# Queries of the dilation-4 pattern: from projections inside attention to seven half-size block products ahead of it

## Chip, core and metric

The kernel runs on one core of a Trainium2 chip. The metric is the device time of one execution in microseconds (us), and smaller is better. All inputs and outputs are float32. TensorE (PE in the profile) multiplies, ScalarE (ACT) and VectorE (DVE) do the elementwise work, GpSimd (POOL) and SyncE (SP) mostly issue DMA transfers.

## What is computed

Two decoder layers, 1024 tokens wide and 1024 features deep. The first layer mixes tokens with a gated MLP, the second with dilated sliding-window attention; each is followed by an MLP of width 4096 with a squared ReLU. The change touches the attention layer alone. Cut to that:

```python
B_HEADS, B_HEAD_DIM = 16, 64
B_PATTERNS = ((128, 1), (512, 4), (2048, 16))          # (window, dilation), numbered g = 0, 1, 2

def mixer_b(h, w_qkv, w_out, slopes):
    qkv = (h @ w_qkv).reshape(B, S, N_PAT, 3, B_HEADS, B_HEAD_DIM)
    for g, (window, dilation) in enumerate(B_PATTERNS):
        o, lse = dilated_branch(qkv[:, :, g, 0], qkv[:, :, g, 1], qkv[:, :, g, 2], window, dilation, slopes)
        ...
    wts = softmax(stack(lses)); o = sum(wts * stack(outs))
    return o.reshape(B, S, 1024) @ w_out

def dilated_branch(q, k, v, window, dilation, slopes):
    ...                                   # tokens are split by residue modulo the dilation, 128 per block
    s = einsum(q, k and the previous block's k) * E ** -0.5 + ALiBi bias, masked
    m = max(s); p = exp(s - m); l = sum(p)
    return (p / l) @ v, m + log(l)
```

For each of the three patterns there is a q, a k and a v, each a product of h (1024 x 1024) with 1024 columns of `w_qkv`. So there are nine such products: (g, X) with X = 0 for q, 1 for k and 2 for v.

## The kernel before, in words

**Split numbers.** To keep float32 accuracy every operand of a large product is cut in two tiles of a faster PE type, a rounded `hi` (an ACT cast, line 111) and the rest `lo` (a DVE subtraction, line 112); the helper is `split`. A product then takes three matmuls: hi by hi, hi by lo, lo by hi.

**Stage "values".** Five of the nine products are made by `values` before attention starts: v of all three patterns, and q and k of pattern 0. Each is cut into half-size blocks and made by seven block products in place of eight (Strassen's scheme in Winograd's form): `V_STEPS` lists (g, X, p) with p the product's number. One entry of `V_STEPS` is 4 row blocks m x 4 k tiles x 3 terms = 48 matmuls with 512 columns each (line 1502). `RightForms.prepare` loads and splits the weight block of the next entry; `evict` takes a finished sum out of PSUM. Products 1, 5 and 6 are only kept for later sums; 2, 3, 4 and 7 give a quarter of the result each. A finished quarter of v is split and written to `v_dram`, one of q or k to `qk_dram`, 512 KB a block, by a DMA from POOL's queue (line 1474), and attention reads it back.

**Stage "attention".** For each pair of heads hp (eight pairs) and each pattern in the order 2, 1, 0, `attend` puts the work into numbered slots, eight slots to a pattern, so that a pair takes 24. A slot has two positions, here called half slots. In a pattern's slots: scores (PE, tile `sc`), then `soften`: bias and minimum on DVE (line 1728, tile `p`) and the exponential on ACT (line 1730); transposes of the probabilities on PE (tile `pT`); `halve`, a cast on ACT and a subtraction on DVE that split the transposed probabilities (`pThi`, `pTlo`); and `weighted`, the product with v (tile `pv`), three half slots behind the transposes. `merge` weighs the three patterns' results of an earlier pair on DVE (tile `bc`). The stretch of pattern 0 carries most of this DVE work.

**Projections inside attention.** The other four products, q and k of patterns 2 and 1, are made pair by pair by the generator `project`: a unit is one (pattern, q or k) of one pair, 2 halves x 8 steps, and a step is three matmuls with 512 columns (line 1605, tiles `psq` and `psk`). At a unit's start `cut` splits the next unit's 128x1024 weights (tiles `wqk_hi`, `wqk_lo`), at each half's end the sum is split into `qhi`/`qlo` or `khi`/`klo`. `lead` steps run before slot 0. After that a running credit lets out a step now and then, after the attention work of a half slot:

```python
credit += 512 - lead
while credit >= 351:
    credit -= 351
    next(stream, None)
```

With 512 steps in all and a lead of 56 that is 456/351 = 1.30 steps a half slot. These steps are what PE does while ACT and DVE work on scores and probabilities. The scheduler places instructions by its own estimates near the place where the slots issue them, and every engine takes its instructions in a fixed order.

**After the last pair's projections** the first products with the output weights (`out_begin`, tile `psoa`) take their place, from slot 176 on.

## Time and profile before

| | |
|---|---|
| median of 3 runs | 2651.45 us (2650.08 to 2653.6) |
| the profiled execution | 2647.53 us, of which the span of its instructions is 2645.8 |
| granted TensorE clock | 0.999 of full speed |
| PE busy | 2624.9 us, 99% of the span, 13016 matmuls |
| DVE busy | 1982.6 us, 75% |
| ACT busy | 1397.5 us, 53% |
| stage "values" | from 943.3 us of the span to 1331.2 |
| stage "attention" | from 1331.2 to about 1985 |

"Busy" is the time in which an engine had an instruction in work; matmuls overlap in the pipeline, so a busy PE says that it had no hole, not that it ran at its peak. The chain is followed back from the last instruction to what released each step. A row with `[1.46 <-ACT p L1730]` says that the engine sat idle for 1.46 us before this instruction, and that the ACT instruction of line 1730 ended the wait. In a window's row the number in brackets counts instructions. Tiles carry the names of the program without numbers.

### The profile page before, as it was taken

The page shows a single profiled execution, that of the slowest core. Times are in us where ns is not written, and L with a number is a line of the kernel's source. Part 1 is how long each engine was busy: PE and PEld are TensorE (multiplying, and loading weights), DVE is VectorE, ACT ScalarE, POOL GpSimd, SP SyncE. Part 2 cuts the span into 40 slices and gives each one's busy share as a digit, 9 for nine tenths or more (in the row PEclk, how much of TensorE's full clock was granted, in tenths as well). Part 3 has the DMA queues.
Part 4 walks back from the last instruction along what each step waited for, and adds up shares of the span by engine and source line. Part 5 has one row for each costly group of instructions (what it writes and reads, how often), then busy time and mean ns, then how long its engine had stood idle before and what let it go on. Part 6 is the DMA issues. An engine that isn't in the chain of part 4 may idle for free.

```text
span 2645.8 us, 36898 instructions
## 1 busy us (share of the span) xinstructions
PE 2624.9 (99%) x13016; PEld 2183.0 (83%) x13016; DVE 1982.6 (75%) x3558; ACT 1397.5 (53%) x2639; POOL 110.2 (4%) x190
## 2 busy tenths in 40 slices
PE   8999999999999999999999999999999999999998
PEld 6888888888888878888888888888888888888887
DVE  6886898886988887646647777777669965687887
ACT  5454475555444554343436666666657655554432
POOL 0000000000000001111110000000010000000000
PEclk9999999999999999999999999999999999999999
DMA  8543367778867546555576655665893654495562
GB/s 299 187 121 118 128 198 238 241 235 283 315 215 243 190 159 231 190 184 191 175 217 165 169 157 142 159 156 155 251 247 120 212 191 147 154 324 185 180 207 88
DMA packets 351794, 513.74 MB, mean 194 GB/s; under 512 B 60140, under 2 KB 185684, under 8 KB 351608
## 3 DMA queue, kind: packets, MB, share of 16 engines
q1 hardware_dynamic: 335176, 452.61, 54.9%
q0 software_dynamic: 16432, 58.76, 6.2%
q8 instruction: 102, 1.67, 0.3%
q14 instruction: 84, 0.69, 0.1%
HBM read 374.34 MB, written 136.95 MB: 193 GB/s over the span
## 4 chain that ended last, share of the span: by engine, by line
PE 94%; DVE 3%; DMA 1%; ACT 1%; issue 0%; SPq 0%; POOL 0%; DVEq 0%; ACTq 0%; POOLq 0%
PE psd L1154 23%; PE psua L987 13%; PE psv L1502 13%; PE psq L1605 7%; PE psk L1605 7%; PE psuc L987 7%; PE psd_wout L432 3%; PE psu L774 3%; PE psub L987 3%; PE psv L528 3%; PE pv L1788 3%; PE sc L1708 2%; PE pT L1761 2%; PE sc L1704 1%; PE psoa L1992 1%; PE pT L1764 1%
## 5 line engine op out<-in xcount | busy, mean ns | idle before, releaser
L987 PE MATMUL psua<-right,left 128*128 128x512 f32 x1536 | 362.8, 390 | 0.1
L1154 PE MATMUL psd<-rhi,lhi 128*128 128x512 f32 x880 | 342.9, 390 | 0.0
L1154 PE MATMUL psd<-rhi,llo 128*128 128x512 f32 x880 | 342.1, 389 | 0.0
L1154 PE MATMUL psd<-rlo,lhi 128*128 128x512 f32 x880 | 342.0, 389 | 0.0
L987 PEld LDWEIGHTS psua<-right,left 128*128 128x128 f32 x1536 | 287.2, 188 | 61.3 <-DVE left L112 0.7
L1730 ACT ACTIVATE p<-p,stat 128x128 f32<-128x128 f32 (+1 forms) x384 | 168.7, 441 | 70.8 <-DVE stat L1728 69.7
L1154 PEld LDWEIGHTS psd<-rhi,lhi 128*128 128x128 f32 x880 | 165.2, 188 | 35.1 <-ACT part L1018 0.9
L1154 PEld LDWEIGHTS psd<-rhi,llo 128*128 128x128 f32 x880 | 165.2, 188 | 34.1
L1154 PEld LDWEIGHTS psd<-rlo,lhi 128*128 128x128 f32 x880 | 165.2, 188 | 33.9
L987 PE MATMUL psuc<-right,left 128*128 128x512 f32 x768 | 186.5, 390 | 0.0
L987 PEld LDWEIGHTS psuc<-right,left 128*128 128x128 f32 x768 | 143.7, 188 | 30.3 <-DVE right L112 0.6
L112 DVE TENSOR_TENSOR pTlo<-pT,pThi 128x512 fp32r<-128x512 f32 (+1 forms) x160 | 99.6, 622 | 69.3 <-ACT pThi L111 67.5
L112 DVE TENSOR_TENSOR left<-ws,left 128x512 fp32r<-128x512 f32 x128 | 88.0, 689 | 81.7 <-ACT left L111 79.9
L112 DVE TENSOR_TENSOR llo<-lraw,lhi 128x1024 fp32r<-128x1024 f32 x112 | 136.2, 1218 | 2.3 <-ACT lhi L111 2.3
L1605 PE MATMUL psk<-form_L,wqk_hi 128*128 128x512 f32 x384 | 126.3, 410 | 0.0
L1605 PE MATMUL psq<-form_L,wqk_hi 128*128 128x512 f32 x384 | 125.1, 406 | 0.0
L111 ACT CAST lhi<-lraw 128x1024 fp32r<-128x1024 f32 x112 | 117.0, 1048 | 11.8 <-PE psd L1154 6.7
L111 ACT CAST pThi<-pT 128x512 fp32r<-128x512 f32 (+1 forms) x160 | 84.9, 530 | 71.6 <-PE pT L1761 51.9
L111 ACT CAST left<-ws 128x512 fp32r<-128x512 f32 x128 | 79.2, 620 | 79.6 <-DVE ws L911 69.0
L1502 PE MATMUL psv<-vrhi,form_S 128*128 128x512 f32 x384 | 119.8, 390 | 1.3 <-DVE vpart L1467 0.9
L1728 DVE CUSTOM_DVE_ANT_0 p<-sc,bias 128x128 f32<-128x128 f32 (+1 forms) x384 | 113.8, 346 | 9.0 <-PE sc L1708 5.4
L138 DVE SCALAR_TENSOR_TENSOR adaacc<-adaw,silu_c,adaacc 128x512 f32<-128x512 f32 x140 | 104.5, 747 | 7.3 <-DMA adaw<-in_ada_w_dram 6.2
(369 smaller groups left out, 6099.4 us busy)
## 6 DMA issues: line engine op xcount, KB each, us to landing
lraw<-forms SPq DMA_DIRECT2D x112, 512.0 KB
adaw<-in_ada_w_dram SPq DMA_DIRECT2D x160, 256.0 KB
up<-in_mlp_w_up_dram SPq DMA_DIRECT2D x64, 512.0 KB
forms<-s SPq DMA_DIRECT2D x128, 256.0 KB
rraw<-in_mlp_w_down_dram SPq DMA_DIRECT2D x64, 512.0 KB
forms<-part SPq DMA_DIRECT2D x96, 256.0 KB
v<-vs POOLq DMA_DIRECT2D x48, 512.0 KB, 3.6
vraw<-in_b_w_qkv_dram SPq DMA_DIRECT2D x42, 512.0 KB
```

The costliest lines, as they stand in the source:

```text
L111: first = A.copy(hi, src) if hi_engine is A else hi_engine.tensor_copy(hi, src)
L112: return first, lo_engine.tensor_tensor(lo, src, hi, op=ALU.subtract)
L138: ins = V.scalar_tensor_tensor(acc[:], raw[:], silu_c[:, k : k + 1], acc[:], ALU.mult, ALU.add)
L432: T.matmul(p[:], stat[a][:, k, o : o + P], u[b][:, w], start=n == 0, stop=n == count - 1)
L528: ins = T.matmul(sums[i][:], hT[half][a_][:, k, o : o + P], units[c, k // 2][b_][:, n : n + HALF], start=k + a_ + b_ == 0, stop=k == KD - ...
L774: T.matmul(p[:], wu[a_][:, k * P : (k + 1) * P], hT[half][b_][:, k, :], start=k + a_ + b_ == 0, stop=k == KD - 1 and a_ == 1)
L987: T.matmul(acc, w[:, a, k, :], right[p][:, b, k, :], start=p in (1, 2, 5) and k + a + b == 0, stop=k == 3 and a == 1, skip_group_check=True)
L1154: ins = T.matmul(sums[kind, m][:, w], l[a][:, k, m * P : (m + 1) * P], r[b][:, k, w], start=p in (1, 5, 2, 3) and kp + k + a + b == 0 or b ...
L1502: T.matmul(acc, rows[:, m * P : (m + 1) * P], cols_, start=p in (1, 2, 5) and kp + k + a + b == 0, stop=kp == 1 and k == 1 and a == 1, ski ...
L1605: T.matmul(p[:], wu[a][:, k * P : (k + 1) * P], h_op(k, half, b), start=k + c_ == 0, stop=k == KD - 1 and c_ == 2)
L1728: V.tensor_tensor_reduce(out=pr, in0=banks[e][:, sl], in1=st["bias"][:, width - w :], scale=-0.125, scalar=3e38, op0=ALU.add, op1=ALU.min, ...
L1730: A.activation(pr, pr, AF.Exp, bias=nm, scale=-1.0, accum_out=l)
```

## The change

q of pattern 1 moves from `project` to `values`. It becomes a sixth product of seven entries in `V_STEPS`, (1, 0), between v of pattern 0 and q of pattern 0. Its quarters are split in the order of residues that pattern 1 uses (`"p (i r) -> p r i"`) and written to a third plane of `qk_dram`. In attention, `load_q` fetches the two halves (128 x 1024 each, `qhi` and `qlo`) seven slots before the pair's pattern 1 starts, on SP's queue, and `place_of` finds a tile's columns in the stored order. `project` is left with six units for two pairs where it had eight: 384 steps, a lead of 48, and 336/348 = 0.97 steps a half slot.

```diff
-    qk_dram = dram.tile([N_PAIRS, 2, P, 2, S], F32, name="qk_0")
+    qk_dram = dram.tile([N_PAIRS, 3, P, 2, S], F32, name="qk_0")
...
-    V_STEPS = [(g, X, p) for g, X in ((2, 2), (1, 2), (0, 2), (0, 0), (0, 1)) for p in (1, 2, 5, 6, 7, 4, 3)]
+    V_STEPS = [(g, X, p) for g, X in ((2, 2), (1, 2), (0, 2), (1, 0), (0, 0), (0, 1)) for p in (1, 2, 5, 6, 7, 4, 3)]
...
-                    t = (work if m % 2 else parted).tile([P, 2, HALF], F32R, name=f"qs_{X}_{p}_{m}", **where)
-                    split(t[:, 0], t[:, 1], acc)
-                    nc.gpsimd.dma_start(qk_dram[4 * dh + m, X, :, :, half * HALF : (half + 1) * HALF], t[:].bitcast(F32))
+                    t = (work if m % 2 else parted).tile([P, 2, HALF], F32R, name=f"qs_{g}_{X}_{p}_{m}", **where)
+                    hi, lo = t[:, 0], t[:, 1]
+                    if g == 1:
+                        hi, lo, acc = (z.rearrange(way, r=4) for z, way in ((hi, "p (r i) -> p r i"), (lo, "p (r i) -> p r i"), (acc, "p (i r) -> p r i")))
+                    split(hi, lo, acc)
+                    nc.gpsimd.dma_start(qk_dram[4 * dh + m, X + 2 * g, :, :, half * HALF : (half + 1) * HALF], t[:].bitcast(F32))
...
-                todo = [(n, X) for n in range(len(order)) if order[n][1] for X in range(2)]
+                todo = [(n, X) for n in range(len(order)) if order[n][1] for X in range(order[n][1] % 2, 2)]
...
+                if g == 1:
+                    @at(max(0, base - 7), 1)
+                    def load_q():
+
+                        for i, m in enumerate(("qhi", "qlo")):
+                            t = my[m] = qk[1].tile([P, S], F32R, name=f"{m}_{hp}_{g}", tag=m)
+                            nc.sync.dma_start(t[:].bitcast(F32), qk_dram[hp, 2, :, i, :])
...
-                                T.matmul(banks[e][:, sl], q_[a][rows, tq], k_[b][rows, keys],
+                                T.matmul(banks[e][:, sl], q_[a][rows, tq if g == 2 else place_of(t)], k_[b][rows, keys],
...
+                def place_of(t):
+                    start = (t % 2) * HALF + (t // 2) * P
+                    return slice(start, start + P)
...
-            lead, credit = 7 * KD, 0
+            lead, credit = 6 * KD, 0
...
-                    credit += 512 - lead
-                    while credit >= 351:
-                        credit -= 351
+                    credit += 384 - lead
+                    while credit >= 348:
+                        credit -= 348
```

Over the whole program PE has 9373 rows of instructions before and 9345 now, and 13002 and 12954 matmuls in them. How the change moves instructions shows at three places.

**PE, pattern 0 of the third pair** (heads 4 and 5), from the last group of scores on (`sc_4_0_3`, `sc_5_0_3`). `psq`/`psk` are projection steps, `pv` the products with v. Before:

```order
L1704 MATMUL sc_5_0_3_14128<-bk_2_3_14037,bq_2_3_14036 128x256 x2
L1605 MATMUL psq_3_1_0_14081<-form_L22_8464,wqk_14_hi_13710 128x512 x2
L1605 MATMUL psq_3_1_0_14081<-form_L22_8464,wqk_14_lo_13711 128x512
L1605 MATMUL psq_3_1_0_14081<-form_L22_8464,wqk_14_hi_13710 128x512 x2
L1605 MATMUL psq_3_1_0_14081<-form_L22_8464,wqk_14_lo_13711 128x512
L1788 MATMUL pv_4_0_0_14161<-pThi_4_0_0_14106,v_2_0_13873 128x256
```

Now:

```order
L1715 MATMUL sc_5_0_3_14465<-bk_2_3_14380,bq_2_3_14379 128x256 x2
L1608 MATMUL psk_3_1_1_14366<-form_L12_7979,wqk_11_hi_14068 128x512 x2
L1608 MATMUL psk_3_1_1_14366<-form_L12_7979,wqk_11_lo_14069 128x512
L1803 MATMUL pv_4_0_0_14497<-pThi_4_0_0_14443,v_2_0_14225 128x256
L1803 MATMUL pv_4_0_0_14497<-pTlo_4_0_0_14444,v_2_0_14225 128x256
```

Two projection steps stood between these scores and the next product with v, and one stands there now. The transposes that need these scores' exponentials (`pT_4_0_2`) follow one more step behind, in both.

**SP's queue, the load of q for the third pair.** Names are tiles and the tensors in memory. Before, at the place where the weights of the fourth pair's q of pattern 1 were fetched:

```order
L1673 DMA bq_1_3_13093<-qk_0_118 64x2x256 x2
L1582 DMA wq_3_1_raw_13236<-in_b_w_qkv_dram 128x8x128
L1671 DMA bk_2_0_13750<-qk_0_118 64x2x256 x2
L1899 DMA o_dram_11204<-bc_0_2_12581 128x1024
L1650 DMA v_2_2_13256<-v_2_117 64x8x256
```

Now, where the stored q of the third pair is fetched:

```order
L1684 DMA bq_1_2_13411<-qk_0_118 64x2x256 x4
L1661 DMA qhi_2_1_13742<-qk_0_118 128x1024
L1661 DMA qlo_2_1_13744<-qk_0_118 128x1024
L1647 DMA v_1_0_13343<-v_0_115 128x8x256
L1838 DMA st_dram_11737<-stat_1_1_13074 128x8x4
```

The loads of a pair's q stand in the queue among the second pair's pattern 0, ahead of that pattern's v (`v_1_0`); the weight load is gone.

**PE, the last pair (heads 14 and 15), where the projections end.** Before:

```order
L1761 MATMUL pT_14_2_0_18244<-ident_76,p_14_2_2_18026 128x128 x2
L1605 MATMUL psk_7_1_0_18227<-form_L22_8464,wqk_31_hi_17803 128x512 x2
L1605 MATMUL psk_7_1_0_18227<-form_L22_8464,wqk_31_lo_17804 128x512
L1605 MATMUL psk_7_1_0_18227<-form_L22_8464,wqk_31_hi_17803 128x512 x2
L1605 MATMUL psk_7_1_0_18227<-form_L22_8464,wqk_31_lo_17804 128x512
```

Now:

```order
L1608 MATMUL psk_7_1_0_18184<-form_L22_8464,wqk_23_lo_17709 128x512
L1776 MATMUL pT_14_2_0_18326<-ident_76,p_14_2_0_18098 128x128 x2
L1776 MATMUL pT_14_2_0_18326<-ident_76,p_14_2_2_18119 128x128 x2
L1776 MATMUL pT_14_2_1_18360<-ident_76,p_14_2_4_18256 128x128 x2
L1776 MATMUL pT_14_2_1_18360<-ident_76,p_14_2_6_18292 128x128 x2
L1719 MATMUL sc_14_1_0_18370<-khi_7_1_18010,qhi_7_1_18157 128x128
L1803 MATMUL pv_14_2_0_18350<-pThi_14_2_0_18335,v_7_2_18040 128x128
```

The last projection now ends ahead of these transposes, and no projection step stands between them, the first scores of pattern 1, and the product with v that needs their split.

## Prediction

> **What bounds the kernel now.** I read the page's busy line and chain first, then the table of windows for the stage "values" and for one whole pair of attention (the third), then the longest piece of the chain there and the list of what PE waited for between 1331 and 2022 us.

> ```profile
> span 2645.8 us, 36898 instructions
> PE 2624.9 (99%) x13016; PEld 2183.0 (83%) x13016; DVE 1982.6 (75%) x3558; ACT 1397.5 (53%) x2639; POOL 110.2 (4%) x190
> PE 94%; DVE 3%; DMA 1%; ACT 1%; issue 0%; SPq 0%; POOL 0%; DVEq 0%; ACTq 0%; POOLq 0%
> 1179.00:1255.00 76.00, 76.00 (x337) 62.94 (x336) 43.98 (x50) 31.63 (x43) 10.61 (x16) 1.00 0.56 191
> 1255.00:1331.00 76.00, 76.00 (x337) 62.90 (x337) 45.96 (x56) 33.26 (x47) 13.20 (x19) 1.00 0.57 198
> 1532.54:1605.76 73.22, 73.22 (x486) 62.92 (x486) 53.98 (x166) 48.19 (x143) 3.04 (x6) 1.00 0.58 153
> 1331.37 10.88 PE psq L1605 x48
> PE pT L1764 <- ACT p L1730: 1.5, 1, 1.5
> PE pst L893 <- ACT h L897: 0.3, 1, 0.3
> ```

> A window's columns are its bounds and length, then the busy time of PE, PEld, DVE, ACT and POOL, the granted clock, the DMA share and GB/s. PE is the chain (94%), and in both stages it is busy for the whole window at a clock of 1.00. In all of attention it waited once, 1.5 us, for an exponential. So matmuls taken out are time taken out, as long as ACT and DVE still deliver. The piece of 48 matmuls with 512 columns in 10.88 us gives 0.2267 us for one, and 0.68 for a projection step of three. The two windows of "values" give 152 / 674 = 0.2255: the same price.

> **The matmuls.** Attention loses q of pattern 1: 8 pairs x 2 halves x 8 steps x 3 = 384 matmuls, 384 x 0.2267 = 87.04 us. "Values" gains seven products of 48: 336 x 0.2267 = 76.16 us. The balance is 48 matmuls, -10.88 us. The other 12954 stay.

> **What the added products bring to "values".** Rows of the tile that they fill, of its stores, and of the slowest DVE operation there is with a strided operand:

> ```profile
> L1502 PE MATMUL psv<-form_L,vrhi x192: 389/389/389, 1178.9 to 1319.9; 128*128 128x512 f32 x192
> L1474 POOL DMA_DIRECT2D qk<-qs x32: 675/681/707, 1195.9 to 1335.0; - x32
> 1541.90 1.09 DVE L1884 TENSOR_TENSOR bc<-oT,bc 128x512 f32<-128x512 f32 x1 [1.65 <-DMA bc<-w_dram]
> ```

> All 192 matmuls of that form, in q and k of pattern 0, take 389 ns with no spread: the stage runs at PE's pace. Those two windows are two such products, and the new one repeats their work, so its splits, sums and copies fall in a stretch where DVE has 76 - 46 = 30 us idle and ACT 43. The split in residue order has strides. Its 16 subtractions cost between 0.69 us (the plain price, below) and 1.09 (the strided row) each, so 6.4 us more at most, in 30 of idle time. Sixteen more stores of 512 KB on POOL's queue come at the rate at which 32 went out in the 152 us, DMA share 0.57. Cost: nothing, covered by matmuls; without that cover the worst case is the 6.4 us.

> **What attention loses beside matmuls.** The third pair's stretch of pattern 0 is the densest, and I cut it in five windows:

> ```profile
> 1550.80:1556.90 6.10, 6.10 (x47) 5.14 (x47) 4.14 (x15) 3.79 (x14) 0.81 (x2) 1.00 0.14 29
> 1556.90:1563.00 6.10, 6.10 (x40) 5.30 (x39) 5.42 (x13) 3.04 (x7) 0.00 (x0) 1.00 0.53 151
> 1563.00:1569.10 6.10, 6.10 (x39) 5.36 (x38) 5.61 (x14) 5.16 (x14) 0.00 (x0) 1.00 0.64 190
> 1569.10:1575.20 6.10, 6.10 (x40) 5.36 (x39) 5.58 (x15) 5.10 (x14) 0.00 (x0) 1.00 0.74 196
> 1575.20:1581.30 6.10, 6.10 (x40) 5.36 (x39) 4.53 (x14) 4.71 (x13) 0.00 (x0) 1.00 0.59 190
> L111 ACT CAST qhi<-psq x32: 559/578/589, 1336.9 to 1886.0; 128x512 fp32r<-128x512 f32 x32
> L112 DVE TENSOR_TENSOR qlo<-psq,qhi x32: 679/691/693, 1337.5 to 1886.7; 128x512 fp32r<-128x512 f32 x32
> 1564.27 1.22 DVE L112 TENSOR_TENSOR wqk_lo<-wk_raw,wqk_hi 128x1024 fp32r<-128x1024 f32 x1
> 1562.49 1.06 ACT L111 CAST wqk_hi<-wk_raw 128x1024 fp32r<-128x1024 f32 x1 [0.44 <-PE sc L1704]
> 1579.01 0.69 DVE L112 TENSOR_TENSOR pTlo<-pT,pThi 128x512 fp32r<-128x512 f32 x1 [1.50 <-ACT pThi L111]
> ```

> The DVE sum is 25.28 of 30.5 us, the ACT sum 21.80. Per pair the change removes 48 matmuls, two `qhi`/`qlo` and one weight split: on PE 10.88 us, on DVE 2 x 0.69 + 1.22 = 2.60, on ACT 2 x 0.58 + 1.06 = 2.22. Spread evenly, the stretch has 30.5/73.2 of that. PE's time there becomes 30.5 - 4.53 = 26.0, DVE's work 25.28 - 1.08 = 24.2 (93%), ACT's 21.80 - 0.92 = 20.9. So PE stays the longest, but by 1.8 us only, where DVE's idle time was 5.2. Part of that idle time lies behind PE and shrinks with it; part, like the 1.50 us before the last row, is DVE standing in its order behind an ACT result. If just that 1.50 stays, DVE needs 25.7 of 26.0 and nothing stalls. If all 5.2 stays, 29.4 against 26.0: a stall of 3.4 us. These are the ends for one pair.

> Inside that stretch the tightest place is the fourth transpose of a pack right behind the last scores. Here it is in the third pair, with two projection steps before the products with v, and in the seventh, with one:

> ```profile
> 1579.47 1.20 PE L1704 MATMUL sc<-bk,bq 128*128 128x256 f32 x8
> 1581.66 0.41 DVE L1728 CUSTOM_DVE_ANT_0 p<-sc,bias 128x256 f32<-128x256 f32 x1
> 1582.12 0.51 ACT L1730 ACTIVATE p<-p,stat 128x256 f32<-128x256 f32 x1 [1.77 <-DVE stat L1728]
> 1583.40 0.27 PE L1764 MATMUL pT<-ident,p 128*128 128x128 f32 x1
> ...
> 1873.89 1.20 PE L1704 MATMUL sc<-bk,bq 128*128 128x256 f32 x8
> 1876.31 0.51 ACT L1730 ACTIVATE p<-p,stat 128x256 f32<-128x256 f32 x1
> 1877.12 0.27 PE L1764 MATMUL pT<-ident,p 128*128 128x128 f32 x1
> ```

> In the third pair the exponential is done at 1582.63 and the transpose comes at 1583.40: slack 0.77. The order shows one step fewer there now, 0.68 us, which leaves 0.1. The seventh pair already stands at one step: done at 1876.82, transpose at 1877.12, slack 0.3 and no wait. But both DVE rows come at their times after a stretch of DVE work, and that stretch is to be shortened by 4.5 us against 1.1 of work. So I expect small waits, between 0 and 3.4 us a pair. The seventh pair's row is the nearest and speaks for the low end; I take 0.5, in each of the seven pairs that still have projections: +3.5 us. I leave the one wait of before as it is:

> ```profile
> 1431.19 1.20 PE L1704 MATMUL sc<-bk,bq 128*128 128x256 f32 x8
> 1432.16 1.05 ACT L111 CAST wqk_hi<-wq_raw 128x1024 fp32r<-128x1024 f32 x1 [1.98 <-PE sc L1704]
> 1434.93 0.41 DVE L1728 CUSTOM_DVE_ANT_0 p<-sc,bias 128x256 f32<-128x256 f32 x1
> 1435.39 0.51 ACT L1730 ACTIVATE p<-p,stat 128x256 f32<-128x256 f32 x1 [1.21 <-DVE stat L1728]
> 1436.04 0.33 PE L1764 MATMUL pT<-ident,p 128*128 128x128 f32 x1 [1.46 <-ACT p L1730]
> ```

> It is the first pair, at the same place with one step. A weight split waited 1.98 us on ACT, the casts behind it in ACT's order came late, DVE waited for those with `qlo` and `pTlo`, and the bias step stood behind them: 3.74 us from scores to bias where the third pair had 2.19. This is how a 1.5 us stall arises with ACT and DVE far from full.

> [...]

> **The last pair's end of projections.** In the order, the last steps no longer stand between its first transposes and the products with v that need their split. Three rows of the third pair give that chain:

> ```profile
> 1536.73 0.60 PE L1761 MATMUL pT<-ident,p 128*128 128x128 f32 x4
> 1537.42 0.59 ACT L111 CAST pThi<-pT 128x512 fp32r<-128x512 f32 x1 [0.66 <-PE pT L1761]
> 1538.04 0.69 DVE L112 TENSOR_TENSOR pTlo<-pT,pThi 128x512 fp32r<-128x512 f32 x1 [0.57 <-ACT pThi L111]
> ```

> From the transposes' start to the end of `pTlo` it is 2.0 us, and 0.6 of it is the transposes themselves. Scores of pattern 1 cover some of the rest. The ends are 0 and 2.0; I take 1.0.

> **Queues.** The two 512 KB loads of q go on SP's queue seven slots ahead, 7 slots of 62.3/24 us with the shorter pairs, 18 us. No row shows such a load; the store of the same size, by the page's group of DMA issues, and a chain of two small DMAs bound it from below and above:

> ```profile
> qk<-qs POOLq DMA_DIRECT2D x32, 512.0 KB, 4.3
> 1531.59 0.35 DVE L1863 TENSOR_TENSOR ma<-ma,mal 128x16 f32<-128x16 f32 x3
> ```

> A store lands 4.3 us after issue; the merge's way through memory and back takes from 1531.94 to 1541.90, 10 us. Two loads one behind the other are 8.6 to 10 us, in 18: hidden. What stands behind them on SP, v of pattern 0, is used a pattern (62.3/3 = 21 us) later. If the cover were gone, first scores of pattern 1 would wait. The merge row itself waits 1.65 us now and would wait some 1.5 longer with shorter slots; that is DVE at a place with idle time, and costs nothing.

> **Sum.** -87.04 + 76.16 + 3.5 + 1.0 = -6.4 us against the profiled execution of 2647.53 us, so 2641.1. That execution lies 3.9 us under the median of 2651.45, and I apply the difference to the median: 2645.0. No change can be told from noise within 0.2%, 5.3 us.

> **Rivals.**
> 1. Full gain. The seventh pair's slack of 0.3 speaks for it: all pairs then stand at one step without a wait, and the first pair's 1.46 may go, as one split fewer stands in ACT's order. -10.9 to -12.3: 2639 to 2640.5.
> 2. My forecast, stalls of 0 to 1 us a pair: -10.9 to -3.
> 3. Small stalls grow: 1.2 to 1.6 us a pair, as in the first pair, with the last pair's 1: 7 x 1.4 + 1 = 10.8, no change, 2651.
> 4. Slower: DVE becomes the bound of pattern 0's stretch. Its idle time behind ACT stays whole, 3.4 us a pair: 7 x 3.4 + 1 - 10.9 = +13.9, 2665. It decides from 10.88 / 7 = 1.55 us a pair. The windows at 5.4 to 5.6 of 6.1 speak for it; that of the three pairs that run with one step there (first, fourth, seventh) only the first stalls, against.

> That the change moves nothing on PE is excluded: the order holds 48 matmuls fewer.

> **How the numbers follow.** Forecast 0.5, full gain 0.2, small stalls 0.2, slower 0.1. The forecast is the second, 2645.0; alone it ranges 2640.5 to 2648.5. A range from 2639 to 2652 holds the first three but for their tails, 0.85, and leaves the fourth out. Faster by over 5.3 us: all of the first and 0.35 of the second's 0.5, 0.55. Slower by as much: the fourth and no more, 0.1. Within: 0.35.

> **What would show it.** "Values" longer by 76 us with no hole in PE; a pair's period of 73.22 - 10.88 = 62.3 plus its stall; PE rows of the fourth transpose behind the last scores of pattern 0 with waits of 0 to 1 us on ACT's exponentials; a wait of PE on `pTlo` in the last pair; no wait on `qhi` or `qlo`. I am wrong if pairs take 64 us or more (the third and fourth rivals), if "values" grows by over 77, or if scores of pattern 1 wait for a DMA.

## The result and the profile after

The changed kernel takes 2662.57 us in the median of six runs (2657.89 to 2663.86), the kernel before 2649.34 beside it (six runs, 2647.74 to 2653.6). The ratio is 1.0046, with a 95% interval of 1.0033 to 1.0059: it is slower by some 12 us, where 6.4 less were forecast. The profiled execution is the quickest of the six, 2657.89 us, 10.4 over that of before; the trace readings that follow account for those 10.4. Why the other five take 4 to 6 us more isn't recorded: their mean clocks are the same (0.998 and 0.999).

The page after, its span, busy line and chain:

```profile
span 2656.2 us, 36952 instructions
PE 2622.6 (99%) x12968; PEld 2175.2 (82%) x12968; DVE 2006.8 (76%) x3584; ACT 1416.2 (53%) x2657; POOL 115.8 (4%) x206
...
PE 85%; DVE 6%; ACT 3%; DMA 3%; issue 1%; SPq 0%; POOL 0%; DVEq 0%; ACTq 0%; POOLq 0%
```

PE's share of the chain fell from 94% to 85%. DVE, ACT and DMA took the difference: PE now waits. By windows, three of "values" (the first is the added product), then two middle pairs and the step from the seventh pair to the last, each from the first scores of pattern 0 to the next pair's:

```profile
1178.00:1254.00 76.00, 76.00 (x337) 62.94 (x336) 46.95 (x49) 36.14 (x43) 10.61 (x17) 1.00 0.56 192
1254.00:1330.00 76.00, 76.00 (x337) 62.91 (x336) 46.61 (x53) 32.11 (x43) 11.04 (x17) 1.00 0.57 197
1330.00:1406.00 76.00, 76.00 (x337) 62.94 (x336) 44.84 (x55) 32.62 (x47) 13.17 (x19) 1.00 0.56 193
1607.64:1671.80 64.16, 62.99 (x440) 53.98 (x439) 50.81 (x163) 46.42 (x140) 2.19 (x6) 1.00 0.73 196
1671.80:1736.61 64.81, 63.68 (x444) 54.38 (x442) 51.05 (x164) 45.81 (x140) 2.22 (x6) 1.00 0.67 173
1865.34:1937.07 71.73, 69.25 (x459) 59.05 (x457) 50.32 (x165) 45.10 (x141) 4.58 (x8) 0.98 0.99 271
```

"Values" paid 76.2 us and has no hole. Attention got back 66.8 us in place of 87.0. Where the other 20.3 went, by the matmuls that the order leaves out of each stretch, at 0.2267 us:

| stretch (from first scores of pattern 0 to the next pair's) | before | now | matmuls alone would give | lost |
|---|---|---|---|---|
| from the end of "values" to the first pair's | 81.1 | 68.8 | 68.2 | 0.6 |
| first to second pair | 75.1 | 66.9 | 64.9 | 2.1 |
| second to seventh pair, five periods | 367.7 | 323.0 | 312.6 | 10.5 |
| seventh to last pair | 75.2 | 71.7 | 66.4 | 5.3 |
| last pair's pattern 0, to the first `psod` (output products) | 43.5 | 45.3 | 43.5 | 1.8 |

With 0.8 us gained ahead of "values" and 1.8 lost behind attention: -0.8 + 76.2 - 66.8 + 1.8 = +10.4.

What PE waited for in attention and behind it, waits over 0.15 us (in before one of 1.5 us stood there, and one of 0.3). `bq` and `bk` are q and k of pattern 0, read back from memory; `stat` is the minimum that the bias step leaves for the exponential:

```profile
PE pT L1779 <- ACT p L1745: 4.9, 5, 1.7
PE pv L1803 <- DVE pTlo L112: 4.8, 12, 1.0
PE pv L1803 <- ACT pThi L111: 1.5, 3, 1.1
PE sc L1715 <- DMA bq<-qk: 0.8, 1, 0.8
PE pst L893 <- ACT acc L274: 0.8, 1, 0.8
PE sc L1715 <- issue: 0.6, 1, 0.6
```

Twenty waits on transposed or exponentiated probabilities, of 0.15 to 1.7 us, of two kinds. Up to the first `psod` all waits make 13.4 us, 12.0 more than before; with 1.7 us for a lower clock (below) that is 13.7 of the 20.3. The other 6.6 us stand in no wait of this list. The first kind stands at pattern 0's last scores, here in the second pair (DVE, ACT and PE rows in order of time):

```profile
1557.67 1.20 PE L1715 MATMUL sc<-bk,bq 128*128 128x256 f32 x8
1558.95 0.68 DVE L112 TENSOR_TENSOR bc<-bc,bc 128x512 fp32r<-128x512 f32 x1
1559.66 0.69 DVE L1813 TENSOR_TENSOR oT<-oT,pv 64x512 f32<-64x512 f32 x1
1560.38 0.69 DVE L112 TENSOR_TENSOR klo<-psk,khi 128x512 fp32r<-128x512 f32 x1
1560.99 0.68 DVE L112 TENSOR_TENSOR pTlo<-pT,pThi 128x512 fp32r<-128x512 f32 x1
1561.59 0.41 DVE L1743 CUSTOM_DVE_ANT_0 p<-sc,bias 128x256 f32<-128x256 f32 x1
1562.05 0.51 ACT L1745 ACTIVATE p<-p,stat 128x256 f32<-128x256 f32 x1 [1.51 <-DVE stat L1743]
1562.70 0.33 PE L1779 MATMUL pT<-ident,p 128*128 128x128 f32 x1 [1.17 <-ACT p L1745]
```

The scores are ready at 1558.87. DVE takes four other operations ahead of the bias step, without a gap, and that step starts 2.7 us later; PE has two projection steps and a product with v for that time, and then waits. The second kind stands between a transpose and the product with v that needs its two halves, here behind the first pair:

```profile
1506.96 0.39 PE L1803 MATMUL pv<-pThi,v 128*128 128x256 f32 x1 [1.10 <-ACT pThi L111]
1507.80 0.39 PE L1803 MATMUL pv<-pTlo,v 128*128 128x256 f32 x1 [0.46 <-DVE pTlo L112]
```

Two things make it new. One is the cover: the PE work between the last transpose of a group of three or four and the first use of their low half, counted at 0.2267 us for 512 columns. At the tightest place of a pattern it was usually 2.78 us in pattern 2, 3.34 in pattern 1 and 3.46 in pattern 0. In the first seven pairs it is 2.10 to 2.83, 1.98 to 2.66 and 2.78 now, mostly one projection step (0.68) less. (The figures in the expectations below are up to 0.3 higher; the differences are the same.) The other is the chain through ACT and DVE. It takes 2.0 us when nothing is in its way, 1.4 of it behind the last transpose, and the cover left would still have done for that, but for one place in the last pair. At the twelve places where PE waited, it took 2.6 to 6.1 us, and 2.0 to 4.4 at the same places before: the cast or the subtraction stood behind other work in its engine's order. The 1.10 us above follow an idle ACT and then eight exponentials in a row; the longest wait on `pTlo`, 1.03 us at 1595.17, follows a DVE that had waited for the merge weights:

```profile
1502.76 0.40 ACT L1745 ACTIVATE p<-p,stat 128x128 f32<-128x128 f32 x1 [3.92 <-DVE stat L1743]
...
1592.26 1.06 DVE L1899 TENSOR_TENSOR bc<-oT,bc 128x512 f32<-128x512 f32 x1 [3.22 <-DMA bc<-w_dram]
```

The last pair has both, and something else. PE's rows there, and the granted clock in windows of 5 us:

```profile
1905.36 0.39 PE L1608 MATMUL psk<-form_L,wqk_lo 128*128 128x512 f32 x1
1905.59 1.04 PE L1776 MATMUL pT<-ident,p 128*128 128x128 f32 x8
1906.81 0.32 PE L1719 MATMUL sc<-khi,qhi 64*128 64x128 f32 x1 [0.19 <-ACT khi L111]
1907.30 0.33 PE L1803 MATMUL pv<-pThi,v 128*128 128x128 f32 x1 [0.17 <-ACT pThi L111]
...
1908.25 0.33 PE L1803 MATMUL pv<-pTlo,v 128*128 128x128 f32 x1 [0.16 <-DVE pTlo L112]
...
1910.49 0.79 PE L2007 MATMUL psoa<-wo_hi,oTs 128*128 128x512 f32 x1
```

```profile
1905.00:1910.00 5.00, 4.48 (x37) 3.65 (x35) 3.41 (x10) 3.27 (x9) 0.40 (x1) 0.96 1.00 363
1910.00:1915.00 5.00, 5.00 (x23) 4.11 (x21) 2.13 (x13) 2.63 (x12) 0.00 (x0) 0.70 1.13 254
```

After the last projection PE has only small pieces of work for 4 us, some of them behind short waits, 0.5 us in all. Then the granted clock falls, and a `psoa` matmul (output product) takes 0.79 us. (0.04 + 0.30) x 5 = 1.7 us are lost by the clock alone.

### The profile page after: what moved, and what is told of

It reads as the page before. It is cut to its first block, busy times and chain, and to the rows that moved or that the text cites. A ratio compares the mean times of both kernels' runs of the same rounds, so it can differ in the third digit from the quotient of the medians.

```text
span 2656.2 us, 36952 instructions
## 1 busy us (share of the span) xinstructions
PE 2622.6 (99%) x12968; PEld 2175.2 (82%) x12968; DVE 2006.8 (76%) x3584; ACT 1416.2 (53%) x2657; POOL 115.8 (4%) x206
## 4 chain that ended last, share of the span: by engine, by line
PE 85%; DVE 6%; ACT 3%; DMA 3%; issue 1%; SPq 0%; POOL 0%; DVEq 0%; ACTq 0%; POOLq 0%
PE psd L1154 23%; PE psv L1505 16%; PE psua L987 13%; PE psuc L987 7%; PE psk L1608 4%; PE psd_wout L432 3%; PE psu L774 3%; PE psub L987 3%; PE psv L528 3%; PE psq L1608 2%; PE pv L1803 2%; ACT p L1745 2%; PE sc L1719 1%; PE pT L1776 1%; DVE pTlo L112 1%
## 5 line engine op out<-in xcount | busy, mean ns | idle before, releaser
L1154 PE MATMUL psd<-rlo,lhi 128*128 128x512 f32 x880 | 342.0, 389 | 0.0
L112 DVE TENSOR_TENSOR left<-ws,left 128x512 fp32r<-128x512 f32 x128 | 87.9, 688 | 81.0 <-ACT left L111 79.2
L112 DVE TENSOR_TENSOR llo<-lraw,lhi 128x1024 fp32r<-128x1024 f32 x112 | 136.1, 1218 | 2.3 <-ACT lhi L111 2.3
L112 DVE TENSOR_TENSOR pTlo<-pT,pThi 128x512 fp32r<-128x512 f32 (+1 forms) x160 | 98.9, 619 | 39.0 <-ACT pThi L111 37.4
L111 ACT CAST lhi<-lraw 128x1024 fp32r<-128x1024 f32 x112 | 117.1, 1048 | 11.5 <-PE psd L1154 6.7
L111 ACT CAST left<-ws 128x512 fp32r<-128x512 f32 x128 | 79.2, 620 | 81.9 <-DVE ws L911 70.1
L1505 PE MATMUL psv<-form_S,vrhi 128*128 128x512 f32 x384 | 118.1, 389 | 0.0
L111 ACT CAST rhi<-rraw 128x1024 fp32r<-128x1024 f32 x48 | 50.5, 1052 | 110.9 <-issue 64.5
## 6 DMA issues: line engine op xcount, KB each, us to landing
lraw<-forms SPq DMA_DIRECT2D x112, 512.0 KB
up<-in_mlp_w_up_dram SPq DMA_DIRECT2D x64, 512.0 KB
rraw<-in_mlp_w_down_dram SPq DMA_DIRECT2D x64, 512.0 KB
vraw<-in_b_w_qkv_dram SPq DMA_DIRECT2D x50, 512.0 KB
v<-vs POOLq DMA_DIRECT2D x48, 512.0 KB, 3.6
```

Source lines behind the costliest of these rows:

```text
L111: first = A.copy(hi, src) if hi_engine is A else hi_engine.tensor_copy(hi, src)
L112: return first, lo_engine.tensor_tensor(lo, src, hi, op=ALU.subtract)
L1154: ins = T.matmul(sums[kind, m][:, w], l[a][:, k, m * P : (m + 1) * P], r[b][:, k, w], start=p in (1, 5, 2, 3) and kp + k + a + b == 0 or b ...
L1505: T.matmul(acc, rows[:, m * P : (m + 1) * P], cols_, start=p in (1, 2, 5) and kp + k + a + b == 0, stop=kp == 1 and k == 1 and a == 1, ski ...
```

## Experiments

In the experiments, as in the changed kernel, the period of a middle pair is the mean of the five from the second pair to the seventh. It is 64.6 us in the changed kernel; from before, with the matmuls taken out, it would be 62.5.

**Is it the transfers, or DVE's load?** Theory A made DVE's work and order responsible, theory B the added transfers. Two kernels that each leave something out:

```diff
-steps = [lambda f=f, g=g, half=half: f(g, half) for f, g in pieces for half in range(2)]
+steps = [(lambda f=f, g=g, half=half: f(g, half)) if f is cut or hp > N_PAIRS - 3 else (lambda: None) ...]
```

> The multiplications and additions of the merge are left out in the first six pairs (ten of twelve DVE operations, some 8 us of DVE a pair; the split of the merged rows and all transfers stay). Theory A: both DVE waits go, pair periods fall from 64.4-65 to 62.3-63, 10 to 13 us in six pairs, and the last pair keeps its 5 us: 2649 to 2653 us, ratio 1.000 to 1.0015. Theory B (transfers): nothing changes, 2662, ratio 1.0046.

```diff
 for i, m in enumerate(("qhi", "qlo")):
+    if hp:
+        my[m] = got[1][m]
+        continue
     t = my[m] = qk[1].tile(...)
     nc.sync.dma_start(...)
```

> The loads of the stored q are left out for all pairs but the first, whose q tiles the others use; nothing else changes. Theory B (the added transfers slow attention): pair periods fall from 64.4-65 towards 62.3, 8 to 12 us in all, ratio 1.000 to 1.0015. Theory L: pairs two to seven keep their waits and periods, only the waits for bq and bk of the last pair go, 1 to 4 us: ratio 1.003 to 1.0045.

Without the q loads: 2660.55 us, ratio 1.0032 (1.0016 to 1.0049), period 64.6. The waits are those of the changed kernel, place by place:

```profile
PE pv L1806 <- DVE pTlo L112: 5.0, 12, 0.9
PE pT L1782 <- ACT p L1748: 4.9, 5, 1.7
PE pv L1806 <- ACT pThi L111: 1.5, 3, 1.1
```

Theory B is out for the middle pairs. The wait for `bq` in the last pair, which I expected to go, stays at 0.8 us as well. Without the merge's arithmetic: 2658.74 us, ratio 1.0024 (1.0013 to 1.0035), period 64.3. In the period that is a sixth of what theory A asked for. The waits on the exponential fall to 1.9 us, but those on the halves stay:

```profile
PE pv L1803 <- DVE pTlo L112: 4.8, 13, 0.5
PE pT L1779 <- ACT p L1745: 1.9, 4, 0.9
PE pv L1803 <- ACT pThi L111: 1.7, 4, 1.1
```

So DVE's load alone doesn't account for the periods either.

**Moving work about.** Three single moves against theory A's three places: the merge a slot later (`pace * n + 24` for 22), the projection steps dealt out by pattern, and the output products two slots earlier.

> All twelve merge steps of a pair start one slot later. Theory A: the 3.2 us wait of DVE for the merge weights shrinks to under 1 us and the waits of the product with v on pTlo in pattern 1 go, some 0.5 to 1 us a pair; one or two merge steps more fall into pattern 0, so its waits on the exponential may grow by as much. 2656 to 2664 us, ratio 1.002 to 1.006; what decides is the list of waits, not the time. Theory B: pair periods and waits stay as they are, 1.0046.

2665.64 us, ratio 1.0044 (1.0029 to 1.0059), period 64.4. DVE's wait of 3.2 us for the merge weights is gone altogether. With it went PE's wait of 1.03 us behind it, and that period fell from 65.3 us to 64.0; but other waits came in their place, and the sums are nearly what they were: 4.9 us on the exponential, 4.4 on `pTlo`. So place two of theory A is real, at one place, and small. The time went up in the last pair instead: PE waits 4.0 us for `bq` there, the clock falls for 6.8 us, and its pattern 0 takes 48.2 us for 45.3.

```diff
-credit += 384 - lead
-while credit >= 348:
-    credit -= 348
+credit += 12500 if n < 168 and n // 8 % 3 == 2 else 8240
+while credit >= 10000:
+    credit -= 10000
```

> The projection steps of attention are dealt out unevenly: 1.25 a half slot in pattern 0, 0.824 elsewhere, with the same total. Theory A (the lost time is three local waits: DVE's order at pattern 0's last scores, DVE's order behind the first merge multiply, and a hole with a low clock in the last pair): the waits on the exponential at pattern 0's end go, about 1.1 us in each of six pairs, while the wait behind the merge multiply grows, since its memory round trip of 10 us meets shorter slots; 2656 to 2661 us, ratio to the kernel before 1.002 to 1.004. Theory B (the added loads and stores slow everything a little): pair periods stay at 64.4 to 65, ratio 1.0046.

2661.27 us, ratio 1.0032 (1.002 to 1.0044), period 66.0. The waits on the exponential fell from 4.9 us to 0.6, but those on `pThi` grew from 1.5 to 5.6, in the patterns that got fewer steps. Four times the waits on `pThi` and then `pTlo` add up to 1.4 or 1.5 us there, and three of these holes were followed by a low clock of 0.50; the period with the longest of them is 69.9 us.

```diff
-if n >= last_group - 8:
-    due += 6
-    while due >= 8:
-        due -= 8
+if n >= last_group - 10:
+    due += 2
+    while due >= 3:
+        due -= 3
 ...
-@at(last_group - 9, 0)       # rows_first
+@at(last_group - 12, 0)
-@at(last_group - 8, 1)       # rows_second
+@at(last_group - 11, 1)
```

> The first products with the output weights start two slots earlier and run at 0.667 a half slot instead of 0.75; the loads of their rows start three slots earlier. They then stand between the last pair's first transposes and the products with v. Theory A: the hole in the last pair and its 5 us at a granted clock of 0.70 go, 4 to 5.5 us: 2657 to 2659 us, ratio 1.0025 to 1.003. Rival: the clock falls for another reason than PE's own hole, then it stays at 0.70 for some us and the gain is under 2 us, ratio above 1.0038.

2662.68 us, ratio 1.0032 (1.002 to 1.0044). The hole at the last projection is gone, with its low clock. In its place PE waits 3.5 us for `v`, whose load now stands behind those of the rows, and the clock falls there (0.996 in the mean of the profile, for 0.998 in the changed kernel): the last pair takes 76.5 us. The time moved.

**Is it the length of the chains?** Theory L: fixed latency, too little cover.

```diff
-    then = half_slot + 3
+    then = half_slot + 4
```

> In all pairs but the last, the product with v comes four half slots behind the transposes in place of three; everything else as changed. By the order this restores the PE work between a transpose and the use of its low half to the values of the kernel before (2.8 us in pattern 2, 2.9 to 3.6 in pattern 1, 3.7 in pattern 0; 2.15, 2.25 to 2.9 and 3.05 without it). Theory L (each chain through ACT and DVE has a fixed length and PE's work between is now too short): the waits of the product with v on pThi and pTlo go, 6.3 us in the profile, and with them clock drops of 2 us; the waits on the exponential (4.9 us) stay: 2655 to 2659 us, ratio 1.0015 to 1.003. Theory A as it was (DVE's load and order): the waits move but stay, ratio above 1.004.

2654.43 us, ratio 1.0018 (1.0009 to 1.0027): some 7 us better than the changed kernel by the ratios (3.4 by the profiled executions), period 63.9. The waits on the halves fell from 6.3 us to 3.6, and no low clock is left in attention (0.999 in the mean of the profile, as before the change). But the waits on the exponential grew, from 4.9 to 7.4:

```profile
PE pT L1779 <- ACT p L1745: 7.4, 8, 1.9
PE pv L1803 <- DVE pTlo L112: 2.7, 6, 0.9
...
PE pv L1803 <- ACT pThi L111: 0.9, 2, 0.4
```

The cover was short; what it freed ran into DVE. The other chain, by earlier scores, `starts = {0: (0, 2, 3, 5), ...}` for all pairs:

> Pattern 0's scores start in slots 0, 2, 3, 5 in every pair, as the last pair has it, in place of 0, 2, 4, 6. Theory L: the waits of the fourth transpose on the exponential go (4.9 us in the profile, 6 with the restarts); the waits on pThi and pTlo stay: 2655 to 2659 us, ratio 1.0015 to 1.003. If DVE's load is what holds (theory A), the wait returns at another place of pattern 0 and the ratio stays above 1.004.

2661.24 us, ratio 1.004 (1.0025 to 1.0055), period 64.9. The waits on the exponential went, as theory L says, and came back ahead of the scores, whose PSUM banks DVE's bias step had not yet read:

```profile
PE pv L1803 <- DVE pTlo L112: 5.0, 13, 0.8
PE sc L1715 <- DVE stat L1743: 2.9, 6, 0.8
```

The two edits together:

> The two shifts together. Theory L: pair periods of 62.3 to 63.2 us, losses left only in the first and the last pair, 8 to 12 us under the changed kernel: 2650 to 2655 us, ratio 0.9995 to 1.0015. Theory A: under 4 us gained, ratio above 1.003.

2658.06 us, ratio 1.0029 (1.0017 to 1.0042), period 64.1: no better than the first alone. The waits on the banks are 4.4 us there; a wait of 3.6 us for `bk` comes in the first pair's pattern 0, and a low clock there and in the last pair takes 5.1 us. Moving the place of a step past DVE's order gave nothing here; theory L alone fails.

**Two limits at once.** Theory LA: cover, and DVE's work in pattern 0; take away either and the other still holds.

The later product and the kernel without the merge's arithmetic, in one:

> The product with v a half slot later, and the merge's multiplications and additions left out in the first six pairs. Theory LA (two limits, of which either alone holds the pair period up: the fixed chain from transposes to the low half, and DVE's work in pattern 0 before the last exponentials): pair periods of 62.3 to 63.2 us where each edit alone left 62.8 to 64.7, the waits on the exponential fall from 7.4 us to under 2.5: 2646 to 2650 us, ratio 0.998 to 1.0005. Theory L alone: the waits on the exponential stay at 5 to 7 us, ratio 1.0015 to 1.002.

2649.69 us, ratio 0.9995 (0.9986 to 1.0005). The period is 62.9 us, 0.4 over the 62.5 that the matmuls alone would give. Alone, the later product left 63.9 and the missing merge 64.3, so 0.7 and 0.3 us gained singly and 1.7 together. The waits:

```profile
PE pT L1779 <- ACT p L1745: 2.5, 6, 1.0
...
PE pv L1803 <- ACT pThi L111: 1.6, 3, 0.9
...
PE pv L1803 <- DVE pTlo L112: 1.2, 3, 0.5
```

This run settles that cover and DVE's work together make the loss of the middle pairs. That either alone holds them up is shown less well: it rests on the periods of one profile of each kernel. By the ratios of the medians the two edits simply add: 1.0046 falls by 0.0028 with the later product, by 0.0022 without the merge's arithmetic, and by 0.0051 with both. What is left to the forecast stands for the most part in the first and the last pair, which these edits hardly touch.

**Versions that leave nothing out.** Each has the later product and one or two edits against DVE's limit.

> The product with v a half slot later, and projection steps at 1.25 a half slot in pattern 0 and 0.824 elsewhere. Theory LA: the first edit gives the sparser patterns their cover back, the second gives DVE time in pattern 0; the waits on the exponential fall to under 3 us and those on pTlo stay under 3: 2647 to 2652 us, ratio 0.9985 to 1.001. If the losses only move, ratio 1.0015 to 1.003.

2655.54 us, ratio 1.0014 (1.0005 to 1.0024), the lowest ratio of all complete versions, not told apart from the later product alone; period 64.4. The waits on the exponential are 1.3 us, those on the halves 6.0. Two periods are 63.2 and 62.3, one is 68.2, with the clock at 0.51 and 0.81 in two windows of 5 us in it.

```diff
-pace = 2 if hp < N_PAIRS - 2 else 1
-    n = pace * n + 22
+    n = n + 24
```

> The product with v a half slot later, and the twelve merge steps packed into half slots 24 to 35 of a pair in place of 22 to 44, so that most stand in pattern 1. Theory LA: pattern 0 loses about 4 us of DVE work, the waits on the exponential fall from 7.4 us to 2 to 4; pattern 1 gets them, with cover of 2.9 us or more: 2648 to 2653 us, ratio 0.999 to 1.0015. If DVE's order in pattern 1 holds instead, waits on pTlo grow by as much and the ratio stays at 1.002.

2666.51 us, ratio 1.0055 (1.004 to 1.007), period 65.3. The waits on the exponential fell from 7.4 us to 5.4, those on the halves grew from 3.6 to 5.2. PE's waits together don't account for a period that is 1.4 us longer; the rest isn't explained.

> All three edits, the fill at 1.12 a half slot in pattern 0 and 0.886 elsewhere. Theory LA: waits of PE in the six middle pairs under 3 us in sum; 2646 to 2651 us, ratio 0.998 to 1.0005. If the losses only move, no better than the better of the two before it.

2657.72 us, ratio 1.0024 (1.0014 to 1.0034): between its parts.

```diff
-in_order(V.tensor_tensor(bc, o, bc, op=ALU.mult))
+in_order((G if hp < N_PAIRS - 2 else V).tensor_tensor(bc, o, bc, op=ALU.mult))
 ...                                                       # the additions likewise
```

> The product with v a half slot later, and the merge's multiplications and additions of the first six pairs on GpSimd in place of VectorE; nothing is left out. Theory LA: DVE has the same load as without the merge, so pair periods of 62.3 to 63.3 us and 2648 to 2651 us, ratio 0.999 to 1.0005. Rival: GpSimd is so slow on 128x512 tiles, or slows VectorE beside it, that the merged rows come late or DVE's own operations get longer: periods of 64 us or more, ratio 1.002 or above.

2664.05 us, ratio 1.0052 (1.0037 to 1.0067), period 65.4. DVE is rid of the merge and its other operations keep their length (`pTlo` 690 ns in both). But a multiplication takes 1.55 us on GpSimd where DVE took 1.06, and an addition 1.30 where it took 0.68, and the next link is on ACT, in its order, ahead of the casts that PE needs (tile `bc`, and ACT's waits from 1475 to 1870 us):

```profile
L1899 POOL TENSOR_TENSOR bc<-oT,bc x36: 1283/1552/1600, 1530.3 to 1866.4; 128x512 f32<-128x512 f32 x36
L1903 POOL TENSOR_TENSOR bc<-bc,bc x24: 1273/1297/1320, 1539.6 to 1871.4; 128x512 f32<-128x512 f32 x24
```

```profile
ACT bc L111 <- POOL bc L1903: 20.3, 9, 4.7
```

So this run doesn't repeat the missing merge: the wait went from DVE to ACT.

The output products two slots earlier as above, with `rows_first` at `last_group - 14` and `rows_second` unmoved:

> The product with v a half slot later, the first products with the output weights two slots earlier, and the load of their first rows five slots earlier (the second rows stay where they were). If the last pair loses by PE's hole and the clock after it: last pair 66 to 67 us in place of 69.5, 2650 to 2652 us, ratio 1.0002 to 1.001. If it loses by transfers that have too little time: the waits for v, bq or bk take over, ratio 1.0018 or above.

2659.43 us, ratio 1.0034 (1.0022 to 1.0047). From the seventh pair on PE waits for `bq` and for a buffer that ACT empties:

```profile
PE sc L1715 <- DMA bq<-qk: 2.4, 1, 2.4
PE sc L1715 <- issue: 2.1, 1, 2.1
PE psoa L2007 <- ACT acc L2016: 2.0, 1, 2.0
```

The rival holds: once the hole is filled, transfers end the last pair, in a window where the DMA share already was 0.99, and the clock falls behind the wait for `bq` for 6.8 us.

> The three edits together. If both causes hold and add up: 2644 to 2648 us, ratio 0.9975 to 0.9990, the first version under the kernel before. If the last pair is bound by transfers: 2648 to 2652, ratio 0.999 to 1.0005.

2669.13 us, ratio 1.0074 (1.0061 to 1.0086): the two failures add up. No complete version beat the kernel before.

## Why the prediction was wrong, point by point

By the profiled executions the sum missed by 16.8 us, +10.4 for -6.4: 10.8 of them in the stalls of the dense stretch, 4.4 at the end of the last pair's projections, 1.6 elsewhere.

- **Values, +76.16.** Right: 1178.1 to 1406.6 is 228.5 us, where 1178.9 to 1331.2 was 152.3, so 76.2, without a hole. Strided splits and stores were covered.
- **Attention's matmuls, -87.04.** The matmuls went, and the price of 0.2267 us was right: with both limits relieved the period is within 0.4 us of it.
- **Stalls in the dense stretch, 0.5 us a pair.** This step failed: 2.1 us a pair in the five middle ones, 12.6 us from the first to the seventh and 1.7 more in the seventh's own pattern 0, so 14.3, where 3.5 were put down for seven. I priced one chain, scores to transposes, at one place, and took the seventh pair's slack of 0.3 us as the nearest row. The same place in that pair now waits 1.7 us. That slack was what DVE's order had left over at the old pace.
- **The chain from transposes to the product with v** was in the prediction, 2.0 us, but for the last pair alone. It stands in every pair: fifteen waits at twelve places, 6.3 us. Its cover could be counted from the order before the run: in pattern 2 2.78 us before, 2.10 in three pairs after. The chain is 2.0 with nothing in its way, but on engines that are 79% (DVE, 50.81 of 64.16 us) and 72% (ACT) busy it often has something in its way. Giving the cover back was worth some 7 us by the ratios.
- **The last pair's end, 1.0 us.** The two last stretches lost 5.3 + 1.8. Of the 5.3, 1.7 are the seventh pair's wait on the exponential, counted above, and 1.7 the lower clock; the waits at the place forecast are 0.5 in sum, and the rest stands among small work around them. Of the 1.8, 1.4 are waits before scores of the last pair's pattern 0, 0.8 of it for the transfer of `bq`. Clock and transfers were not in the sum.
- **Queues.** Right for the q loads: without them nothing changes in the middle pairs. DVE's wait for the merge weights grew from 1.65 us to 3.22, as forecast (1.5 more); its price of nothing was wrong by the one wait of 1.03 us that PE has behind it.
- **Rivals.** The fourth came nearest: slower, 2665, from 1.55 us a pair. The measured 2.1 a pair is beyond that point, the pairs' 64.6 us are over the 64 that the prediction named as a sign of being wrong, and the place is the one named. Its price of 3.4 us a pair was too high and its mechanism half of the truth: DVE's idle time did not all stay, and a second chain and the last pair made up the sum. I gave the case 0.1, because only one of three pairs had stalled at the old pace.

Left open: the 6.6 us of attention's loss that stand in no listed wait, the 1.8 us behind attention (0.8 of it is a wait for `acc`), and the 4 to 6 us by which the unprofiled executions of the changed kernel lie over the profiled one.

## What to carry to other kernels

When filler is taken out between small dependent steps, count the PE work that is left between each producer and its consumer, for every chain in the loop, and set it against the chain's length in the trace. Take the length that the chain has among the engines' other work, not its shortest: here 2.0 us alone, and up to 6.1 where PE waited. A slack seen at the old pace is no slack at the new one. Where two causes lengthen the same period, only the run that relieves both shows that no third is needed.

## What the hardware did that I had not expected

```profile
1508.59:1512.00 3.41, 1.85 (x10) 1.36 (x10) 2.48 (x4) 2.33 (x6) 0.00 (x0) 1.00 1.03 325
1512.00:1515.41 3.41, 3.41 (x14) 3.05 (x13) 0.69 (x1) 1.07 (x2) 0.00 (x0) 0.50 0.38 63
```

```profile
1503.44:1506.86 3.42, 2.42 (x15) 1.71 (x13) 1.37 (x10) 3.42 (x16) 0.00 (x0) 1.00 1.14 240
1506.86:1510.27 3.41, 2.86 (x16) 2.36 (x17) 2.13 (x5) 1.80 (x4) 0.00 (x0) 1.00 1.03 303
```

In the first the whole hole lies in one such window, in the second it is split over two. The first lost 0.50 x 3.41 = 1.7 us by it, the second nothing. One of the two longest falls, in `fill_by_pattern`, comes behind a hole of 1.28 + 0.23 us:

```profile
1715.48:1725.72 10.24, 10.24 (x45) 8.62 (x46) 3.69 (x15) 4.28 (x15) 0.00 (x0) 0.50 0.85 207
```

It cost 0.50 x 10.24 = 5.1 us. The falls last one, two or three times 3.413 us, and where the starts of two in one profile are measured here, they lie whole multiples of it apart. In the changed kernel a second fall begins at 2650.32, behind PE's last matmul: 740.69 us after that of 1909.63, or 217.0 steps. In the six versions that leave nothing out, the granted clock in windows of 5 us gives the starts of two falls each to about 0.1 us; by my estimate from these they are 34.0, 205.0, 217.1, 248.0, 274.0 and 342.0 steps apart. In the pair shown above, where the hole lies on that grid goes with whether the clock falls behind it; no run moved the grid on purpose. With the merge one slot later PE was busy for 1.85 of 3.41 us, its longest gap was 1.1, and that was enough. In the changed kernel the clock stayed at 1.00 behind 2.42 of 3.42 us; in that kernel's last pair PE was busy, with small matmuls, for 2.89 of the 3.41 us before the fall, with no gap over 0.2 us. So busy time alone doesn't decide it, and what does stays open.
